# Earlier W_out weights, a reordered MLP entry, split right-factor buffers, and a rearranged first stage in a one-core transformer block

## The chip, the cores and the metric

The kernel runs on one core of one Trainium2 chip. The metric is device time in microseconds (us) of one execution, the median of several.

## The reference, cut to what matters

One transformer block on x of 1024 x 1024, float32 throughout:

```python
u = rms_norm(h, norm_mix_pre)
(q_n, kc_n, vc_n, ks_n, vs_n, kw_n, vw_n, g_n,
 q_s, k_s, v_s, gate_a, gate_b) = split(u @ w_in)
o_a = nsa_attention(...)          # compressed, selected and window branches
o_b = swa_sink_attention(...)
y = sigmoid(gate_a) * (o_a @ w_up_nsa) + sigmoid(gate_b) * (o_b @ w_up_swa)
h = h + rms_norm(y @ w_out, norm_mix_post)
u = rms_norm(h, norm_mlp_pre)
f = square(relu(u @ w_mlp_in)) @ w_mlp_out      # d_ff = 4096
h = h + rms_norm(f, norm_mlp_post)
```

## The kernel before, in words

TensorE multiplies in a reduced float32 type, so every operand is first split into a high and a low part (`split`: ScalarE rounds and copies, VectorE or GpSimd subtracts), and every product is three matmuls (high by high, high by low, low by high). Weights come from HBM in tiles called `wraw` and become `wh` and `wl`.

The work runs in six stages.

1. **First stage.** `x` comes in eight blocks of 128 rows (`xt`). Each is squared on ScalarE (line 283), scaled by its root mean square and by the norm weights `gB` on VectorE (line 285), transposed by TensorE and split into `uh` and `ul`. `gB` is the weight vector repeated on all partitions by a DMA (`load_bcast`). `v_weights` loads the columns of `w_in` for the values in eight row blocks (`vraw`, two buffers, three DMAs each); `v_block` multiplies a block of `u` by them. All of these loads stand in SyncE's queue.
2. **Projections and attention**, up to the output `o_d`, with the gate columns as filler for TensorE.
3. **Up-projection**, a loop over eight column groups `dc`, whose result `yh`, `yl` lies in pools on the right side of SBUF.
4. **W_out** (`out_proj`): four passes, each for two row blocks and all columns; each pass runs over eight row blocks `k2` of `w_out`, and each `k2` is 12 matmuls. Its weights go through the pool `wp2`, whose space on the left side is that of the attention output `oh_`, `ol_` that the up-projection reads to its last matmul. `norm_a`, `norm_b` and `norm_t` then make the MLP's normed input and transpose it.
5. **MLP entry and first MLP product.** The product is a seven-product (Strassen-Winograd) scheme over 2 x 2 blocks. The right factors `bh[i]`, `bl[i]` are sums of blocks of the input, made by `norm_t` (number 5) and `factor` (3, 6, 4, 7) on VectorE and ScalarE. `head` computes the two products that need only rows 0 to 511 (four `head`s run ahead of the rest, NPRE = 4) and stores `c11` to the DRAM scratch `f_d[0]`. `mlp1(p)` does the other five products of the column pair p (16 pairs); pairs 0 and 1 run interleaved with `factor`. Its left factors are sums of weight blocks: one sum (`sm`, line 1014) and three differences (line 1041) on GpSimd.
6. **Second MLP product** (`product`), again seven products, with split tiles `vh`, `vl`, `fh`, `fl` in the pool `st2` that lies where the right factors were, and the final norm.

The order of each engine's instructions is written at build time by a planner that simulates the engines; among the instructions it holds ready it takes them in the order of the program. `tc.issue_after(ins)` puts the block's instructions behind `ins` on the engine of `ins`. A tile that lies where an earlier tile lay waits until that tile's last reader is done. Queues are in order: an instruction of SyncE that waits holds every DMA behind it.

Of the kernel before, what the change touches and what calls it, by code (L numbers as in the profile page):

```python
# [52 lines left out]
def tile_hybrid_block(ctx: ExitStack, tc: tile.TileContext, x, norm_mix_pre, norm_mix_post, norm_mlp_pre,  # L53
# [27 lines left out]
    def load_bcast(dst, vec):  # L81
        nc.sync.dma_start(dst, bass.AP(tensor=vec.tensor, offset=vec.offset, ap=[[0, P], [1, vec.shape[-1]]]))
# [50 lines left out]
    load_bcast(sink, attn_sinks)  # L133
    nsink = const.tile([P, 8], F32, name="nsink")
    nc.vector.tensor_scalar(nsink, sink, -1.0, None, op0=ALU.mult)
# [36 lines left out]
    with ExitStack() as s_u:  # L172
# [36 lines left out]
        with ExitStack() as s:  # L209
# [12 lines left out]
            for pr, pos in zip(pos_r, (cmp_pos_k, cmp_pos_v)):  # L222
                nc.gpsimd.dma_start(pr, pos[0].rearrange("(a b) d -> a (b d)", b=2))

            def v_weights():
# [17 lines left out]
            with ExitStack() as s0:  # L243
                tp = s0.enter_context(pool("t0"))
                gB = tp.tile([P, D], F32, name="gB")
# [26 lines left out]
                for b in range(NB):  # L272
                    xt = tp.tile([P, D], F32, name="xt", tag="xt", bufs=4)
                    nc.sync.dma_start(xt, x[b * P:(b + 1) * P, :])
                    if b == 0:
                        load_bcast(gB, norm_mix_pre)
# [8 lines left out]
                    nc.vector.scalar_tensor_tensor(u, xt, r, gB, op0=ALU.mult, op1=ALU.mult)  # L285
# [456 lines left out]
    with ExitStack() as s:  # L742
# [3 lines left out]
        yl = [p.tile([P, NB, 512], F32R, name="yl", tag="yl") for p in yp]  # L746
        s_ps = s.enter_context(ExitStack())
        pp = s_ps.enter_context(pool("ps2", space=PSUM))
        ps_any = lambda: pp.tile([P, 512], F32, name="ps", tag="ps", bufs=6)
        with s_ot:  # L750
            dp = s_ot.enter_context(pool("dtmp"))
            for dc in range(8):
# [11 lines left out]
                for c in range(2):  # L764
# [11 lines left out]
                    split(yh[c][:, dc, :], yl[c][:, dc, :], t[0])  # L776
        s_w.close()
# [28 lines left out]
        we = s_we.enter_context(pool("we"))  # L806
        wor = w_out.rearrange("(k p) c -> p k c", p=P)
# [3 lines left out]
        started = []  # L811

        def out_proj(c, ts_, nhs, xs_=(), at=0):
            pss = {(t, nh): ps_any() for t in ts_ for nh in nhs}
            n = 1024 // (512 * len(nhs))
            for k2 in range(NB // n):
                wh, wl = load_w([(None, wor[:, n * k2:n * k2 + n, 512 * nhs[0]:512 * nhs[-1] + 512])],
# [452 lines left out]
```

## Time and profile before

| | |
|---|---|
| median of 3 runs | 1553.06 us (1552.43 to 1554.15) |
| the profiled execution | 1550.25 us |
| its span, first to last instruction | 1548.5 us |
| TensorE (PE) busy in the span | 1475.5 us, 95% |
| VectorE (DVE), ScalarE (ACT), GpSimd (POOL) busy | 1053.7, 788.3, 362.6 us |
| mean granted clock of TensorE | 0.985 of 2.4 GHz |

How to read the rows below. A row of the timeline has the start in us from the span's start, the duration in us, the engine, the line of the kernel, the operation, the tiles (out<-in), the shapes and how many instructions were merged (x8); in brackets stands how long the engine was idle before, and whose end released it. SPq is SyncE's queue. A row of a stretch has its bounds, its length, the busy us of PE, PEld (weight loads), DVE, ACT and POOL with the instructions counted, then TensorE's granted clock as a share, the DMA engines' busy share and GB/s. A row of a group of equal instructions has the line, the engine, the operation, the tiles and shapes, the count, the busy us, the mean ns of one, and the idle time before them.

### The profile page before, as it was taken

The page shows a single profiled execution, that of the slowest core. Times are in us where ns is not written, and L with a number is a line of the kernel's source. Part 1 is how long each engine was busy: PE and PEld are TensorE (multiplying, and loading weights), DVE is VectorE, ACT ScalarE, POOL GpSimd, SP SyncE. Part 2 cuts the span into 40 slices and gives each one's busy share as a digit, 9 for nine tenths or more (in the row PEclk, how much of TensorE's full clock was granted, in tenths as well). Part 3 has the DMA queues.
Part 4 walks back from the last instruction along what each step waited for, and adds up shares of the span by engine and source line. Part 5 has one row for each costly group of instructions (what it writes and reads, how often), then busy time and mean ns, then how long its engine had stood idle before and what let it go on. Part 6 is the DMA issues. An engine that isn't in the chain of part 4 may idle for free.

```text
span 1548.5 us, 19945 instructions
## 1 busy us (share of the span) xinstructions
PE 1475.5 (95%) x6920; PEld 1208.1 (78%) x6920; DVE 1053.7 (68%) x2086; ACT 788.3 (51%) x1525; POOL 362.6 (23%) x290
## 2 busy tenths in 40 slices
PE   6998999999999999999898969899999899999997
PEld 5897888788887788888766757688888688888886
DVE  5555774598855988646547798787667555594775
ACT  5344675598854988654346663233322334334533
POOL 3000342100001000041052035676556300000302
PEclk9999999999999999999999979999999999999999
DMA  7733125111132111174356633444444697353551
GB/s 218 252 98 87 35 50 158 46 35 41 36 99 61 40 35 42 32 257 148 108 192 233 221 116 107 155 148 166 157 137 144 220 359 270 99 194 102 164 176 55
DMA packets 162037, 204.79 MB, mean 132 GB/s; under 512 B 15120, under 2 KB 105264, under 8 KB 161936
## 3 DMA queue, kind: packets, MB, share of 16 engines
q1 hardware_dynamic: 154224, 180.68, 36.8%
q0 software_dynamic: 6992, 20.48, 3.8%
q10 hardware_dynamic: 720, 2.36, 0.4%
q8 instruction: 54, 0.88, 0.2%
q14 instruction: 47, 0.39, 0.1%
HBM read 153.02 MB, written 58.32 MB: 136 GB/s over the span
## 4 chain that ended last, share of the span: by engine, by line
PE 69%; issue 8%; DVE 6%; POOL 3%; DMA 2%; ACT 2%; DVEq 0%; POOLq 0%; ACTq 0%
PE xs L1167 10%; PE ys L1167 8%; PE mm L124 5%; PE mm L126 5%; PE mm L125 5%; PE ps L959 5%; PE ps L961 5%; PE ps L960 5%; PE pt L522 5%; PE o L535 2%; PE o L534 2%; PE s L489 2%; DMA wraw<-in_w_out_dram 2%; PE s L490 2%; PE ps L124 2%
## 5 line engine op out<-in xcount | busy, mean ns | idle before, releaser
L124 PE MATMUL mm<-uh,wh 128*128 128x512 f32 x464 | 200.2, 431 | 5.3 <-DVE qb L448 3.2
L125 PE MATMUL mm<-ul,wh 128*128 128x512 f32 x464 | 183.9, 396 | 0.0
L126 PE MATMUL mm<-uh,wl 128*128 128x512 f32 x464 | 183.7, 396 | 0.0
L91 DVE TENSOR_TENSOR tl<-pt,th 128x512 fp32r<-128x512 f32 x162 | 110.6, 687 | 42.1 <-ACT th L87 41.2
L91 POOL TENSOR_TENSOR wl<-wraw,wh 128x1024 fp32r<-128x1024 f32 x16 | 38.4, 2403 | 417.1 <-ACT wh L87 385.2
L502 ACT ACTIVATE e<-e,nm 128x256 f32<-128x256 f32 (+7 forms) x192 | 124.3, 649 | 20.0 <-DVE nm L496 19.5
L87 ACT ACTIVATE fh<-fraw 128x1024 fp32r<-128x1024 f32 x56 | 59.4, 1063 | 146.1 <-PE xs L1167 78.5
L87 ACT ACTIVATE wh<-wraw 128x1024 fp32r<-128x1024 f32 x69 | 73.1, 1059 | 113.9 <-PE mm L125 36.7
L87 ACT ACTIVATE th<-pt 128x512 fp32r<-128x512 f32 (+1 forms) x178 | 104.4, 593 | 50.6 <-PE pt L522 43.1
L91 DVE TENSOR_TENSOR fl<-fraw,fh 128x1024 fp32r<-128x1024 f32 x56 | 69.3, 1243 | 78.3 <-ACT fh L87 78.3
L1167 PE MATMUL xs<-vl,fh 128*128 128x512 f32 x256 | 100.7, 393 | 4.2 <-DVE vl L91 4.2
L126 PEld LDWEIGHTS mm<-uh,wl 128*128 128x128 f32 x464 | 87.4, 188 | 20.7
L124 PEld LDWEIGHTS mm<-uh,wh 128*128 128x128 f32 x464 | 88.0, 190 | 18.4 <-issue 3.3
L522 PE MATMUL pt<-ident,e 128*128 128x128 f32 x648 | 101.1, 273 | 0.3 <-DVE tl L91 0.2
L91 DVE TENSOR_TENSOR wl<-wraw,wh 128x1024 fp32r<-128x1024 f32 x53 | 69.7, 1315 | 46.0 <-ACT wh L87 45.8
L1167 PE MATMUL xs<-vh,fl 128*128 128x512 f32 x256 | 100.4, 392 | 0.0
L1167 PE MATMUL xs<-vh,fh 128*128 128x512 f32 x256 | 100.1, 392 | 0.0
L125 PEld LDWEIGHTS mm<-ul,wh 128*128 128x128 f32 x464 | 88.3, 190 | 11.9
L522 PEld LDWEIGHTS pt<-ident,e 128*128 128x128 f32 x648 | 80.7, 140 | 18.4 <-issue 0.9
L1190 POOL TENSOR_TENSOR cc<-cc,gB 128x512 f32<-128x512 f32 x14 | 24.3, 1762 | 268.9 <-ACT sq L1189 267.2
L87 ACT ACTIVATE ws_h<-wraw 128x512 fp32r<-128x512 f32 x48 | 30.1, 629 | 107.1 <-PE ps L960 104.8
L959 PE MATMUL ps<-bh,ws_h 128*128 128x512 f32 x192 | 76.3, 397 | 3.9 <-ACT ws_h L87 1.7
(287 smaller groups left out, 4046.4 us busy)
## 6 DMA issues: line engine op xcount, KB each, us to landing
fraw<-f_d SPq DMA_DIRECT2D x48, 512.0 KB, 3.5
wraw<-in_w_mlp_in_dram SPq DMA_DIRECT2D x36, 512.0 KB, 4.4
wraw<-in_w_out_dram SPq DMA_DIRECT2D x32, 512.0 KB, 3.6
f_d<-q SPq DMA_DIRECT2D x64, 256.0 KB, 3.7
b<-in_w_mlp_out_dram SPq DMA_DIRECT2D x32, 512.0 KB, 10.8
wraw<-in_w_in_dram SPq DMA_DIRECT2D x27, 512.0 KB, 4.6
f_d<-c SPq DMA_DIRECT2D x48, 256.0 KB, 4.3
gate_d<-gst SPq DMA_DIRECT2D x32, 256.0 KB, 2.0
```

The costliest lines, as they stand in the source:

```text
L87: nc.scalar.activation(h, src, AF.Copy)
L91: eng.tensor_tensor(l, src, h.bitcast(F32), op=ALU.subtract)
L124: nc.tensor.matmul(ps, ah, bh, start=first, stop=False)
L125: nc.tensor.matmul(ps, ah, bl, start=False, stop=False)
L126: nc.tensor.matmul(ps, al, bh, start=False, stop=last)
L489: nc.tensor.matmul(ps[:, :w], qs[r][:, qcol], kh, start=True, stop=False)
L502: nc.scalar.activation(e[:, :n], e[:, :n], AF.Exp, scale=-1.0, bias=nm[:, r:r + 1], accum_out=sm[:, r:r + 1])
L522: tr = nc.tensor.transpose(pt[:rows, r, :], es[r][:, off:off + rows], ident)
L959: nc.tensor.matmul(ps, ah[:, k, :], bh[i][:, k, :], start=n[0], stop=False, skip_group_check=True)
L960: nc.tensor.matmul(ps, ah[:, k, :], bl[i][:, k, :], start=False, stop=False, skip_group_check=True)
L961: nc.tensor.matmul(ps, al[:, k, :], bh[i][:, k, :], start=False, stop=n[1], skip_group_check=True)
L1167: nc.tensor.matmul(bank[t], l_[:, j, ts], r_[:, j, :], start=a_, stop=z_, skip_group_check=True)
```

## The change

Four groups of edits, of which the first three were joined and the fourth was added.

- **W_out.** Two row blocks of `w_out` are loaded during the up-projection (at dc = 5) into a new pool `wo` on the right side, and the first of them is split there. `out_proj`'s first pass takes them for k2 = 0 and 1; the pool `we` is opened after that pass.
- **MLP entry.** `norm_b(6)` and `norm_b(7)` stand before `norm_t(4)` instead of behind the first `head`; `factor(3, ...)` is put behind `norm_b(7)` on VectorE, and `factor(6, 4, 7)` behind the last subtraction of `norm_t` on VectorE and behind the copy `s1` on ScalarE. The squared ReLU of the four early `c11` moves from VectorE to ScalarE (two steps), and their stores from SyncE's queue to GpSimd's. The raw weights of pairs 0 to 3 are loaded ahead in one sequence, into tiles of `wp2` and `w1a`. The sum and differences of pairs 0 and 1 move from GpSimd to VectorE.
- **Right-factor placing.** Factors 5, 3, 6 lie in a pool of their own (`u1a`), 4 and 7 in `u1`; the split tiles of every fourth step of the second MLP product lie in a new pool `st3`, the others in `st2`.
- **First stage.** Blocks 1 and 2 of `x` go on ScalarE's queue; the norm weights come as one row (`gr`) and are spread to all partitions by two matmuls with a row of ones and two copies; block 0 is scaled in two halves; the value weights come two row blocks at a time and their low parts are all subtracted on VectorE; the sink load moves to GpSimd's queue and its negation to the end of the stage.

```diff
             def v_weights():
-                for k in range(NB):
-                    raw = wp.tile([P, NV], F32, name="vraw", tag="wraw", bufs=2)
-                    nc.sync.dma_start(raw[:, 0:128], wr[:, k, C_VS:C_VS + 128])
-                    nc.sync.dma_start(raw[:, 128:280], wr[:, k, C_VW:C_VW + 152])
-                    nc.sync.dma_start(raw[:, 280:408], wr[:, k, C_VB:C_VB + 128])
-                    split(vh[:, k, :], vl[:, k, :], raw, l_eng="pool" if k % 2 else "dve")
+                for k in range(0, NB, 2):
+                    raw = wp.tile([P, 2, NV], F32, name="vraw", tag="wraw", bufs=2)
+                    for a, b, c in ((0, 128, C_VS), (128, 280, C_VW), (280, 408, C_VB)):
+                        nc.sync.dma_start(raw[:, :, a:b], wr[:, k:k + 2, c:c + b - a])
+                    split(vh[:, k:k + 2, :], vl[:, k:k + 2, :], raw)
...
+                gr = tp.tile([1, D], F32, name="gr")
+                nc.scalar.dma_start(gr, norm_mix_pre)
+                one = tp.tile([1, P], F32, name="one")
+                nc.vector.memset(one, 1.0)
...
-                    nc.sync.dma_start(xt, x[b * P:(b + 1) * P, :])
+                    (nc.scalar if b in (1, 2) else nc.sync).dma_start(xt, x[b * P:(b + 1) * P, :])
                     if b == 0:
-                        load_bcast(gB, norm_mix_pre)
+                        for c in range(2):
+                            cs = slice(c * 512, (c + 1) * 512)
+                            ps = ps_x()
+                            nc.tensor.matmul(ps, one, gr[:, cs], start=True, stop=True)
+                            nc.vector.tensor_copy(gB[:, cs], ps)
...
-                    nc.vector.scalar_tensor_tensor(u, xt, r, gB, op0=ALU.mult, op1=ALU.mult)
+                    for cs in ((slice(0, 512), slice(512, D)) if b == 0 else (slice(0, D),)):
+                        nc.vector.scalar_tensor_tensor(u[:, cs], xt[:, cs], r, gB[:, cs], op0=ALU.mult, op1=ALU.mult)
...
+        def wo_load(k):
+            r = wo.tile([P, 1, 1024], F32, name="wraw", tag="wraw", bufs=2)
+            nc.sync.dma_start(r, wor[:, k:k + 1, :])
+            wo_raw.append(r)
...
+                if dc == 5:
+                    wo_load(0)
+                    wo_load(1)
+                    wo_hl += [wo.tile([P, 1, 1024], F32R, name=n, tag=n) for n in ("wh", "wl")]
+                    split(*wo_hl, wo_raw[0])
...
+        u1a = s_u2r.enter_context(pool("u1a", side="right"))
         u1 = s_u2r.enter_context(pool("u1", side="right"))
         for i in (5, 3, 6, 4):
-            bh[i] = u1.tile([P, 4, 512], F32R, name=f"bh{i}")
+            bh[i] = (u1 if i == 4 else u1a).tile([P, 4, 512], F32R, name=f"bh{i}")
...
+        norm_b(6)
+        norm_b(7)
         norm_t(4)
...
-            nc.vector.scalar_tensor_tensor(c11, c11, 0.0, c11, op0=ALU.max, op1=ALU.mult)
-            nc.sync.dma_start(f_d[0][p], c11)
+            if p < NPRE:
+                nc.scalar.activation(c11, c11, AF.Relu)
+                nc.scalar.activation(c11, c11, AF.Square)
...
+            (nc.gpsimd if p < NPRE else nc.sync).dma_start(f_d[0][p], c11)
...
-        for b in range(4):
-            factor(3, b)
+        with tc.issue_after(last_norm[0].ins):
+            for b in range(4):
+                factor(3, b)
...
+        raws = {p: load_raw(p) for p in range(NPRE)}
...
-            nc.gpsimd.tensor_tensor(sm, a21, a22, op=ALU.add)
+            diff = nc.vector if p < 2 else nc.gpsimd
+            with tc.issue_after(last_t[0].ins):
+                diff.tensor_tensor(sm, a21, a22, op=ALU.add)
...
-                nc.gpsimd.tensor_tensor(o, i0, i1, op=ALU.subtract)
+                diff.tensor_tensor(o, i0, i1, op=ALU.subtract)
...
+        def st_tile(name, kc):
+
+            p, n = (st3, 1) if kc % NG == NG - 1 else (st2, NG - 1)
+            return p.tile([P, 2, 512], F32R, name=name, tag=name, bufs=n)
```

## Rows read from the trace of the kernel before

**Rows 1.** Seven stretches of the span, all engines.

```profile
0.00:42.00 42.00, 27.70 (x119) 22.26 (x120) 24.88 (x57) 22.25 (x46) 12.48 (x18) 0.96 0.78 229
42.00:768.90 726.90, 715.06 (x3667) 597.80 (x3665) 492.42 (x1388) 456.26 (x1021) 95.42 (x94) 1.00 0.29 85
768.90:800.20 31.30, 25.70 (x97) 19.92 (x96) 8.84 (x11) 9.83 (x10) 13.11 (x8) 0.89 0.59 204
...
884.00:907.00 23.00, 22.94 (x104) 18.68 (x105) 22.61 (x46) 17.25 (x35) 1.06 (x2) 1.00 0.57 171
907.00:955.40 48.40, 34.81 (x138) 26.84 (x136) 40.24 (x52) 21.10 (x38) 20.66 (x14) 0.82 0.27 76
955.40:1025.00 69.60, 63.73 (x261) 49.12 (x261) 56.38 (x52) 20.51 (x34) 52.02 (x32) 0.98 0.46 152
...
1227.60:1238.00 10.40, 6.17 (x18) 4.56 (x18) 10.05 (x11) 1.96 (x3) 2.17 (x3) 0.67 0.61 180
```

**Rows 2.** Timeline of the first stage, all engines, us 0 to 42.

```profile
5.48 1.71 SPq L274 DMA_DIRECT2D xt<-in_x_dram  x2
5.49 1.06 ACT L283 ACTIVATE u<-xt 128x1024 f32<-128x1024 f32 x1 [3.25 <-DMA xt<-in_x_dram]
...
7.65 1.29 DVE L285 SCALAR_TENSOR_TENSOR u<-xt,rs_o,gB 128x1024 f32<-128x1024 f32 x1
...
9.08 1.94 PE L161 MATMUL pt<-ident,u 128*128 128x128 f32 x8 [9.08 <-DVE u L285]
...
19.60 0.46 PE L125 MATMUL s<-vl,uh 128*128 128x408 f32 x1 [1.71 <-DVE vl L91]
```

**Rows 3.** The chain that ended last, around the first W_out load.

```profile
768.31 3.94 DMA wraw<-in_w_out_dram
```

**Rows 4.** Timeline of PE in the first W_out pass.

```profile
773.44 2.07 PE L124 MATMUL ps<-wh,yh 128*128 128x512 f32 x4 [4.49 <-ACT wh L108]
...
778.73 1.47 PE L124 MATMUL ps<-wh,yh 128*128 128x512 f32 x4
...
787.50 1.10 PE L124 MATMUL ps<-wh,yh 128*128 128x512 f32 x4
...
790.30 1.10 PE L124 MATMUL ps<-wh,yh 128*128 128x512 f32 x4
```

**Rows 5.** Timeline of the MLP entry: SyncE's queue, GpSimd, VectorE and PE.

```profile
902.73 8.44 SPq L977 DMA_DIRECT2D f_d<-c  x3
...
911.21 34.85 SPq L1010 DMA_DIRECT2D wraw<-in_w_mlp_in_dram  x6
...
915.79 1.26 POOL L1014 TENSOR_TENSOR ws<-wraw 128x512 f32<-128x512 f32 x1 [14.06 <-DMA wraw<-in_w_mlp_in_dram]
...
911.34 1.28 DVE L864 SCALAR_TENSOR_TENSOR o<-hb,rs_o,gpre 128x1024 f32<-128x1024 f32 x1
...
912.76 1.94 PE L874 MATMUL pt<-ident,o 128*128 128x128 f32 x8 [4.72 <-DVE o L864]
...
918.95 0.79 PE L959 MATMUL ps<-bh,s_h 128*128 128x512 f32 x1 [4.25 <-ACT p L1019]
...
923.89 0.79 PE L961 MATMUL ps<-bh,s_l 128*128 128x512 f32 x1 [3.71 <-DVE s_l L91]
```

**Rows 6.** Groups of equal instructions on VectorE and ScalarE, us 884 to 940.

```profile
L91 DVE TENSOR_TENSOR bl<-braw,bh 128x512 fp32r<-128x512 f32 x8 | 7.5, 953 | 0.0
...
L896 DVE TENSOR_TENSOR braw<-b_l,braw 128x512 f32<-128x512 f32 x4 | 2.7, 679 | 0.0
...
L87 ACT ACTIVATE bh<-braw 128x512 fp32r<-128x512 f32 x8 | 4.9, 628 | 1.5 <-DVE braw L899 0.8 <-DVE braw L896 0.6
```

**Rows 7.** Timeline of VectorE and PE at the start of the second MLP product.

```profile
1227.92 0.69 DVE L1056 TENSOR_TENSOR c<-ps,p 128x512 f32<-128x512 f32 x1 [2.50 <-PE ps L961]
...
1229.85 1.22 DVE L91 TENSOR_TENSOR fl<-fraw,fh 128x1024 fp32r<-128x1024 f32 x1
...
1232.26 0.79 PE L1167 MATMUL xs<-vl,fh 128*128 128x512 f32 x1 [4.23 <-DVE vl L91]
```

More of the change, by code (lines that the diff above doesn't have):

```diff
@@ L746, in tile_hybrid_block @@
         yl = [p.tile([P, NB, 512], F32R, name="yl", tag="yl") for p in yp]
+        s_wo = s.enter_context(ExitStack())
+        wo = s_wo.enter_context(pool("wo", side="right"))
+        wor = w_out.rearrange("(k p) c -> p k c", p=P)
+        wo_raw, wo_hl = [], []
+        def wo_load(k):
+            r = wo.tile([P, 1, 1024], F32, name="wraw", tag="wraw", bufs=2)
+            nc.sync.dma_start(r, wor[:, k:k + 1, :])
+            wo_raw.append(r)
         s_ps = s.enter_context(ExitStack())
@@ L816, in out_proj @@
             for k2 in range(NB // n):
-                wh, wl = load_w([(None, wor[:, n * k2:n * k2 + n, 512 * nhs[0]:512 * nhs[-1] + 512])],
-                                [n, 512 * len(nhs)], *((wp2, 2) if not started else (we, WEB)), cut=CUT[c], rpool=wp2, l_eng="dve" if c else None)
+                if started or k2 > 1:
+                    wh, wl = load_w([(None, wor[:, n * k2:n * k2 + n, 512 * nhs[0]:512 * nhs[-1] + 512])],
+                                    [n, 512 * len(nhs)], *((we[0], WEB) if started else (wp2, 2)), cut=CUT[c],
+                                    rpool=wp2, l_eng="dve" if c else None)
+                elif k2:
+                    wh, wl = (wp2.tile([P, 1, 1024], F32R, name=n_, tag="w" + n_[1], bufs=2) for n_ in ("wh", "wl"))
+                    split(wh, wl, wo_raw[1])
+                else:
+                    wh, wl = wo_hl
                 if k2 == at:
@@ L830, in out_proj @@
                                 k == 0, k == NB - 1)
+            if not started:
+                s_wo.close()
+                we.append(s_we.enter_context(pool("we")))
             started.append(1)
@@ L882, in norm_t @@
             t1 = eh.tile([P, 4, P], F32, name="t1", tag="hb", bufs=2)
-            nc.vector.tensor_tensor(t1, pts[0], braw[b % 4, 0], op=ALU.subtract)
+            last_t[0] = nc.vector.tensor_tensor(t1, pts[0], braw[b % 4, 0], op=ALU.subtract)
             nc.scalar.activation(b12[:, :, bs], pts[0], AF.Copy)
@@ L985, in tile_hybrid_block @@
                 norm_t(5)
-                norm_b(6)
-                norm_b(7)
             if p == 1:
@@ L1002, in ab, with load_raw @@
                     p_.tile([P, 4, P], F32R, name=tag + "l", tag=tag + "l", bufs=bufs))
-        def mlp1(p):
-            raw = []
-            for e in range(2):
-                r = wp2.tile([P, NB, P], F32, name="wraw", tag="wraw", bufs=2) if e == 0 else \
-                    w1a.tile([P, NB, P], F32, name="wraw2", tag="wraw2", bufs=2)
-                c0 = (2 * p + e) * P
-                nc.sync.dma_start(r, w_mlp_in[:, c0:c0 + P].rearrange("(k p) c -> p k c", p=P))
-                raw.append(r)
+        def load_raw(p):
+            raw = {}
+            for e in (1, 0):
+                pool_, tag = ((w1a, "wraw2") if e else (wp2, "wraw")) if p > 3 else \
+                    ((wp2, "wraw"), (w1a, "wraw2"), (wp2, "w" + "hl"[e]), (wp2, "w" + "hl"[e]))[p]
+                raw[e] = pool_.tile([P, NB, P], F32, name="wraw", tag=tag, bufs=2)
+                c0 = (2 * p + e) * P
+                nc.sync.dma_start(raw[e], w_mlp_in[:, c0:c0 + P].rearrange("(k p) c -> p k c", p=P))
+            return raw
+        raws = {p: load_raw(p) for p in range(NPRE)}
+        def mlp1(p):
+            raw = raws[p] if p in raws else load_raw(p)
             a11, a12, a21, a22 = raw[0][:, 0:4], raw[0][:, 4:8], raw[1][:, 0:4], raw[1][:, 4:8]
             sm = w1a.tile([P, 4, P], F32, name="ws", tag="ws", bufs=3)
-            nc.gpsimd.tensor_tensor(sm, a21, a22, op=ALU.add)
+            diff = nc.vector if p < 2 else nc.gpsimd
+            with tc.issue_after(last_t[0].ins):
+                diff.tensor_tensor(sm, a21, a22, op=ALU.add)
             early = p in pre
@@ L1077, in tile_hybrid_block @@
                 next(g)
-            for b in range(4 if i else 0):
-                factor(i, b)
+            with tc.issue_after(last_t[0].ins), tc.issue_after(last_s1[0].ins):
+                for b in range(4 if i else 0):
+                    factor(i, b)
         for p in range(2, NPAIR):
@@ L1095, in tile_hybrid_block @@
         st2 = s.enter_context(pool("st2", side="right"))
+        st3 = s.enter_context(pool("st3", side="right"))
+        def st_tile(name, kc):
+            p, n = (st3, 1) if kc % NG == NG - 1 else (st2, NG - 1)
+            return p.tile([P, 2, 512], F32R, name=name, tag=name, bufs=n)
         pq = s.enter_context(pool("ps3", space=PSUM))
```

30 lines of the change are left out of this document (15 added, 15 removed).

## The prediction

> **What bounds the kernel now.** I read the table of stretches first. TensorE (PE) is the bound: in us 42 to 768.9 it is busy 715 of 727 [rows 1]. What a change can win is therefore its idle time and the time it spends at 1.2 GHz, and that sits in few places. The reader is to subtract the first busy figure from the length in each stretch: 14.3 us are idle in the first 42, 5.6 in the first W_out pass (768.9 to 800.2), 13.6 at the MLP entry (907 to 955.4), 5.9 in the pairs behind it, 4.2 at the start of the second MLP product. In three of these the granted clock is also low: 0.89, 0.82 and 0.67 [rows 1]. Then I read each place in the timeline, with the bracket that names who ended the wait.
>
> At full clock a group of 12 matmuls takes 790.30 - 787.50 = 2.80 us [rows 4]. I use this as the price of one W_out row block and of one product of the first MLP product, which are both 12 matmuls of 512 columns.
>
> **W_out.** PE waits 4.49 us for the first weights [rows 4]: their DMA starts only at 768.31, when the attention output under the buffer has been read, and takes 3.94 us [rows 3], then comes the split. After the wait the first 12 matmuls take 778.73 - 773.44 = 5.29 us instead of 2.80 [rows 4]: the clock has fallen, cost 2.5. The stretch of 31.3 us holds eight groups, 8 x 2.80 = 22.4, so at most 8.9 are to be won. The edit puts the first two row blocks into space that nobody holds. PE then goes on at 768.9 without a break for 5.6 us, to 774.5. The third block, which goes the old way, lands when the first one did (768.31 + 3.94 = 772.3) and needs one rounding copy before PE can start: about 773.4, in time. From there on loads and PE run side by side as they do now. That removes the wait (4.5) and the slow start (2.5): **7 us**. Lower bound 4, if the second block's split, which waits for the same old space, makes PE wait some 3 us at 771.7; upper 8.9. The two loads and one split inside the up-projection cost nothing: DMA engines are at 0.29 there and VectorE is busy 492 of 727 us [rows 1]; without that cover it would be the load's 3.9 us.
>
> **MLP entry.** In 907 to 955.4 PE has ten products (five each of pairs 0 and 1), 28.0 us, and two sets of eight transposes, about 2 us together at full clock (half of the 1.94 of the slow one for each [rows 5]). 48.4 - 30 = 18.4 us are lost. Three waits follow each other [rows 5]. The transposes of the last block wait 4.72 us for `norm_b(7)` on VectorE, which starts at 911.34 though PE was through at 907. The first product waits 4.25 and then 3.71 us for its left factor: GpSimd starts the sum at 915.79 because its raw weights were issued at 911.21, and they were issued then because SyncE's queue stood behind three stores of `c11` from 902.73 on. The rest is the low clock.
>
> The edits hit all three. `norm_b(7)` is no longer behind `factor(3)` and `factor(6)`, and can follow its sums: I put it at 897 to 902. The stores leave SyncE's queue, so the raw weights come as soon as a buffer is free, before 907. So the first product can start at about 909. What is late next is VectorE. It is full already: 22.6 of 23.0 us before 907 [rows 1], and it makes all the right factors. The edits take off four squared ReLUs (the shape of the 679 ns row [rows 6], 2.7 us) and put on two sums and six differences (8 x 0.68 = 5.4 us). ScalarE's eight extra steps are 8 x 0.63 = 5.0 us [rows 6] and just fit into the 5.75 us it has idle before 907 [rows 1]. What decides is how long VectorE's steps are: those that ran beside GpSimd's work average 953 ns against 679 [rows 6], 2.2 us for that group alone, and some 8 us over all groups of this kind between 884 and 940 by my estimate from the same ratio over 30 steps. The moved sums take GpSimd's work of pairs 0 and 1 away, but pairs 2 and 3, whose weights now come early, can put GpSimd's work back in the same place. The two ends: VectorE loses 5.3 us of work (- 2.7 + 5.4 - 8) and PE runs almost through, 18 us won; or it gains 2.7, and the right factors are ready no earlier than now, some 936 us, so that PE ends the last two products at about 942 to 945 and the gain is 10 to 13, and less if waits of 4 us each drop the clock again: 6. I take **11 us**, in the lower half, because VectorE's row before 907 shows no room.
>
> The Trainium skill ("SBUF — State Buffer", section "SBUF: two separate sides") has GpSimd and a VectorE step with two SBUF inputs exclude each other for a whole instruction. The 953 against 679 ns agree with that. By it alone, the moved steps take away all of the lengthening and the entry wins 18; with pairs 2 and 3 in their place it wins what rival 1 says.
>
> **The pairs behind.** In 955.4 to 1025 GpSimd is busy 52.0 of 69.6 us, far more than later, and PE idles 5.9 [rows 1]: GpSimd catches up with four pairs at once. With pairs 0 and 1 off it and the weights of 2 and 3 early, part of this goes. Between nothing and 5.9 I take **2 us**.
>
> **Right-factor placing.** PE waits 4.23 us at 1232.26 for `vl`; VectorE begins `fl` only at 1229.85, though it was idle 2.50 us until 1227.92 [rows 7]. The reason I read from the code: in the old placing `fl` lies where factor 7 lies, which the last product reads to its end. In the new one the first three steps' tiles lie on factors 5, 3 and 6, which are free one product (2.8 us) earlier, so `fl` and `vl` (1.22 us each) fit into that 2.50 us gap and behind it. The granted 0.67 over 10.4 us means 6.9 us at 1.2 GHz, 4.2 of them idle; the other 2.7 cost half, 1.3. In all 5.5; I take **5**, bounds 0 (the planner leaves them behind the last pair's sums) and 5.5.
>
> **First stage.** PE starts at 9.08: `x` lands, ScalarE starts at 5.49, and the scaling takes 1.29 before the transposes [rows 2]. Halving it for block 0 gives 0.6, and one load ahead of `x` less in SyncE's queue some 0.4. Blocks 1 and 2, issued at 5.48 so far [rows 2], go out in the first 3 us; the later idle time is 14.3 - 9.1 = 5.2, of which 1.71 is a wait for `vl` [rows 2] that GpSimd and VectorE shared. I take 1 + 2 = **3 us**. The copies of `gB` and the two matmuls lie in PE's and VectorE's empty first 5 us, the larger `vl` steps in VectorE's idle 17 us of 42 [rows 1]. Bounds: 1 + 5.2 = 6 above; below, a loss of 2.3, one block's transfer (0.52 MB at 229 GB/s [rows 1]), if blocks 1 and 2 push the first block back.
>
> The Trainium skill ("Trainium Kernel Development and Optimization", section "Key Constraints") says that DMAs of all queues share the same 16 engines, so a second queue saves only issue time. The DMA share of 0.78 in this stage bears on it but doesn't settle it; by it the term is 1, the sum 26, and rival 2 is the case.
>
> **The sum.** 7 + 11 + 2 + 5 + 3 = 28 us. The profiled execution took 1550.25, 1.75 more than its span and 2.8 less than the median of the runs shown. 1550.25 - 28 = 1522.3; against the median 1553.06 it is 1525.
>
> **The rivals.**
>
> 1. *VectorE takes the waits over at the entry* (0.20). PE starts the first product at 909 and then waits for factors 3 and 6. For it: 22.6 of 23.0 us busy, and 953 ns beside GpSimd. Against: GpSimd's steps of pairs 0 and 1 are gone. The entry wins 3, the pairs behind nothing: 28 - 8 - 2 = 18, 1535.
> 2. *The second queue gains nothing* (0.12). Blocks 1 and 2 delay block 0 by as much as the halves win, and the term of 3 turns to -1: 24 won, 1529. For it: 229 GB/s and 0.78 busy. Against: the repeated `gB` load of 0.52 MB is gone.
> 3. *W_out's loads set the pace anyway, or the early blocks come late* (0.06): the wait moves behind the second block; 28 - 7 = 21, 1532.
> 4. *All the waits go* (0.08): 8.9 + 18 + 5 + 5.5 + 3 = 40, 1513.
> 5. *Slower* (0.03). The planner writes each engine's order anew for the whole program. The place is the attention between 42 and 768.9, where 11.8 us are idle [rows 1]; the price is what a worse order of fillers adds there, and it decides from 28 us on, when that idle time passes 40; at 35 the result would be 1560. Nothing in the diff touches this stage, so little speaks for it.
>
> **How the numbers follow.** The forecast has 0.51, its own range is 1518 to 1532. The range of 8 in 10 takes in rival 4 on one side and most of rival 1 on the other, 1511 to 1539. A difference of 0.2% (3.1 us) is about what a measurement can tell from no change. Faster by more than that holds in all cases but the last, and fails in a tail of rival 1: 0.95; within 0.2%: 0.02; slower: 0.03.
>
> **What would show it.** PE idle at 769 under 1 us and clock 1.00 behind it; the last transposes of `norm_t(7)` before 905, the first product of pair 0 at 909 or so, and no wait over 2 us up to 945; no wait for `vl` at the first xs matmul; the first transposes before 8.5. It would be wrong if VectorE's order puts `norm_b(7)` late again, or if waits of 4 us reappear between the products of pairs 0 and 1.

## The result and the profile after

The changed kernel takes 1532.38 us, the median of 4 runs (1530.81 to 1533.55); the kernel before took 1553.61 us beside it (4 runs, 1552.43 to 1554.35). The ratio is 0.9863, with a 95% interval of 0.9846 to 0.988: 21 us faster. The forecast was 1525 with a range of 1511 to 1539. The time is inside the range, but the sum of 28 us was 7 too high, and it was spread wrongly over the places, with errors both ways that partly cancel.

The two profiled executions have spans of 1548.5 and 1531.3 us, 17.2 apart; the medians differ by more because the profiled execution of before was 3.4 us under its median and that of after 0.7 above. First the stretches of the changed kernel (columns as in [rows 1]). The first keeps the bound of 42 us and the pairs behind the entry keep the length of 69.6 us; the others are cut at the same points of the work as there:

```profile
0.00:42.00 42.00, 35.52 (x152) 27.07 (x153) 29.00 (x71) 22.49 (x44) 7.71 (x15) 1.00 0.85 252
...
763.90:791.10 27.20, 23.38 (x97) 17.62 (x96) 8.63 (x11) 8.74 (x10) 10.08 (x7) 1.00 0.61 207
...
898.90:949.90 51.00, 34.27 (x125) 25.27 (x124) 45.71 (x61) 25.85 (x45) 19.13 (x13) 0.80 0.32 88
949.90:1019.50 69.60, 69.60 (x301) 56.19 (x300) 57.86 (x58) 21.93 (x36) 52.79 (x34) 1.00 0.46 159
1215.30:1225.70 10.40, 10.35 (x39) 8.39 (x40) 10.33 (x13) 3.07 (x3) 1.51 (x3) 0.84 0.77 230
```

The idle time of TensorE (length less first busy figure) went from 14.3 to 6.5 us in the first 42 (3.75 of the difference are the new matmuls that spread the norm weights, before the first transposes), and from 5.9 to nothing in the pairs behind the entry. But at the entry 16.7 us are idle now, 51.0 - 34.27, where 13.6 were, and the clock is 0.80 where it was 0.82. The entry, from which most was forecast, is the place that got worse.

To see where the time came from, I took four points of TensorE's timeline from each trace: the end of the up-projection, the first matmul of the first `head`, the end of the first MLP product, the last `xs` matmul (`xs` are sums of the second MLP product). The lengths between them, in us, for all kernels of this study:

```
                start to end of   W_out, up to    first MLP   second MLP
                up-projection     first head      product     product
before              768.95          114.89         343.97       311.35
after               763.85          110.31         338.89       308.83
undo_first          772.35          109.96         338.37       308.87
undo_wout           765.18          113.64         340.14       307.73
undo_entry          765.68          107.45         343.90       308.03
undo_rf             763.59          109.95         335.32       311.31
sum1_late           764.70          110.06         337.11       307.24
raws23_late         763.66          110.58         336.37       307.51
diffs_pool          764.91          109.13         336.40       308.89
combo               764.60          110.24         336.51       308.01
combo2              764.81          113.07         337.89       307.24
one_queue           763.67          108.34         338.29       308.88
bcast_late          765.08          108.85         338.38       307.24
final3              762.83          108.54         335.35       308.79
```

After less before: 5.1 us from the first stage, 4.6 from W_out, 5.1 from the first MLP product, 2.5 from the second, 17.3 in all. The columns also show what one trace can carry: the same W_out code gives 107.5 to 113.1. Even so the kernels with the old code of a place stand apart: in every column the two longest are before and the kernel that turns that place back (768.95 and 772.35 against 762.8 to 765.7; 114.89 and 113.64 against at most 113.1; 343.97 and 343.90 against at most 340.1; 311.35 and 311.31 against at most 308.9). So each of the four parts earns something; the size of each is known to some 3 us.

**First stage.** The timeline of PE: the first transposes start at 8.51 instead of 9.08 [rows 2], and the wait of 1.71 us for `vl` at 19.60 is gone; the longest that is left is the 0.17 shown.

```profile
8.51 1.09 PE L159 MATMUL pt<-ident,u 128*128 128x128 f32 x4 [1.81 <-DVE rs_r L147]
...
12.36 0.71 PE L125 MATMUL s<-vl,uh 128*128 128x408 f32 x1 [0.17 <-DVE vl L91]
```

**W_out.** The timeline of PE in the first pass, and the chain that ended last there:

```profile
770.74 1.20 PE L124 MATMUL ps<-wh,yh 128*128 128x512 f32 x4 [1.34 <-ACT wh L108]
777.06 1.20 PE L124 MATMUL ps<-wh,yh 128*128 128x512 f32 x4 [0.45 <-ACT wh L108]
784.57 1.20 PE L124 MATMUL ps<-wh,yh 128*128 128x512 f32 x4 [1.64 <-ACT wh L108]
```

```profile
761.45 8.10 DMA wraw<-in_w_out_dram
...
769.63 1.07 ACT wh L108
...
770.76 1.67 POOL wl L116
772.44 3.40 DMA wraw<-in_w_out_dram
```

PE goes on at 763.7 without the wait of 4.49 us and at full clock [rows 4]. But the third row block takes 8.10 us to land, not 3.94 [rows 3], and then two buffers alternate: rounding 1.07, low part 1.67, next load 3.40 and more. The pass takes 27.1 us from its first matmul to the next pass, exactly what it took before, so W_out won the wait and nothing behind it: the slow first group is gone, and waits for loads (3.4 us in the rows above) have its place.

**MLP entry.** The timeline of VectorE, ScalarE and PE:

```profile
899.01 0.68 DVE L1065 TENSOR_TENSOR ws<-wraw 128x512 f32<-128x512 f32 x1
...
903.48 0.83 DVE L1065 TENSOR_TENSOR ws<-wraw 128x512 f32<-128x512 f32 x1 [3.79 <-DMA wraw<-in_w_mlp_in_dram]
904.24 1.88 DVE L930 TENSOR_TENSOR b_l<-b_l,b_h 128x512 f32<-128x512 f32 x3
...
906.04 0.68 DVE L1014 TENSOR_TENSOR c<-ps,s 128x512 f32<-128x512 f32 x1
...
907.41 0.63 ACT L1017 ACTIVATE c<-c 128x512 f32<-128x512 f32 x1
...
907.95 1.08 ACT L1070 ACTIVATE p<-ps 128x512 f32<-128x512 f32 x2
...
908.60 0.80 PE L998 MATMUL ps<-bh,s_h 128*128 128x512 f32 x1 [9.34 <-ACT p L1070]
...
919.29 0.79 PE L998 MATMUL ps<-bh,ws_h 128*128 128x512 f32 x1 [3.46 <-ACT ws_h L87]
...
931.46 6.88 DVE L91 TENSOR_TENSOR bh7l<-braw,bh7h 128x512 fp32r<-128x512 f32 x4
```

Read it backwards from the PE row at 908.60. PE waits 9.34 us for ScalarE's copies `p` (they take the heads' sums out of PSUM, the memory of TensorE's sums, before the first product adds to them). The copies stand behind the two steps of the fourth head's `c11`; these wait for VectorE's add at 906.04; and that stands behind VectorE's sum for pair 1 at 903.48, which waited 3.79 us for a raw weight. Neither the add nor the copies need that weight. The order made them need it.

```profile
895.00:901.00 6.00, 4.26 (x23) 3.33 (x22) 1.98 (x3) 3.62 (x8) 0.55 (x1) 1.00 1.05 285
901.00:907.00 6.00, 0.00 (x0) 0.00 (x0) 3.52 (x6) 1.64 (x4) 2.52 (x2) 0.53 0.92 252
```

```profile
893.15 10.31 DMA wraw<-in_w_mlp_in_dram
```

The two stretches of 6 us and the row of the chain show why the weight is late: the DMA engines are full (shares 1.05 and 0.92), because eight loads of 512 KB for four pairs go out in a row, and this load takes 10.31 us. By the semaphores in the trace (the counters that an instruction waits on) it is the fifth of the eight, though the program has it third; the fourth, which lands at 901.10, is the one that GpSimd's sum for pair 2 waits for. So the order of SyncE's queue has a part in it too.

**Second MLP product.** The wait for `vl` (4.23 us, [rows 7]) is gone, and a shorter one has come:

```profile
1212.85 1.22 DVE L91 TENSOR_TENSOR fl<-fraw,fh 128x1024 fp32r<-128x1024 f32 x1
1213.98 0.68 DVE L1107 TENSOR_TENSOR c<-ps,p 128x512 f32<-128x512 f32 x1
...
1214.70 0.60 ACT L1109 ACTIVATE c<-ps 128x512 f32<-128x512 f32 x1 [0.56 <-DVE c L1107]
...
1215.35 0.74 PE L1224 MATMUL xs<-vh,fh 128*128 128x512 f32 x1 [2.30 <-ACT c L1109]
```

### The profile page after: what moved, and what is told of

Its sections match the earlier page's. It is cut to its first block, busy times and chain, and to the rows that moved or that the text cites. A ratio compares the mean times of both kernels' runs of the same rounds, so it can differ in the third digit from the quotient of the medians.

```text
span 1531.3 us, 19921 instructions
## 1 busy us (share of the span) xinstructions
PE 1472.2 (96%) x6924; PEld 1205.1 (79%) x6924; DVE 1042.8 (68%) x2094; ACT 792.9 (52%) x1529; POOL 343.1 (22%) x281
## 4 chain that ended last, share of the span: by engine, by line
PE 81%; DVE 7%; DMA 6%; ACT 3%; issue 2%; POOL 1%; SPq 0%; DVEq 0%; ACTq 0%; POOLq 0%
PE xs L1224 10%; PE ys L1224 9%; PE mm L124 7%; PE mm L125 7%; PE mm L126 7%; PE ps L1000 6%; PE ps L998 6%; PE ps L999 6%; PE pt L532 5%; DMA wraw<-in_w_out_dram 4%; PE o L545 2%; PE o L544 2%; PE s L499 2%; PE s L500 2%; PE ps L126 2%
```

## The experiments

The changed kernel is the base of all of them; each states its edit.

**One part undone at a time.** Each turns back one of the four groups of the diff and keeps the other three:

```
undo_first:  first stage as before    (v_weights, gr, gB, xt, u, sink)
undo_wout:   W_out as before          (wo, wo_load, wo_hl, we)
undo_entry:  MLP entry as before      (norm_b, factor, c11, load_raw, sm, diff)
undo_rf:     one pool each, as before (u1a, st3)
```

> The changed kernel with its first stage as before. Theory (each part earns where the two traces differ at that place): the 5.2 us that the last x transposes came earlier are kept to the end, because TensorE is the bound from there on; so 1532.4 + 5.2 = 1537.6 us. Prediction's term for this part: 3 us, 1535.4. Rival (the two traces differ there by chance, a gain at the start is swallowed by the attention's fixed order): 1532 to 1533.

> The changed kernel with W_out as before (no early row blocks). Theory: the part earned 4.65 us by the traces, and loads set the pace from the third row block on; so 1532.4 + 4.7 = 1537.1 us, with a wait of about 4.5 us for the first weights and a low clock behind it back in the trace. Prediction's term: 7 us, 1539.4. Rival (loads set the pace anyway, nothing is earned): 1532 to 1533.

> The changed kernel with the MLP entry as before (order, sums, stores, raw weights), the other parts kept. Theory: entry and the pairs behind it together earned only 5.0 us (lost 4.1 at the entry, won 9.1 behind it); so 1532.4 + 5 = 1537.4 us. Prediction's terms: 11 + 2, so 1545.4. Rival (the entry's edit earns nothing once W_out's comes with it): 1532 to 1533.

> The changed kernel with the right factors and the split tiles of the second product in one pool each, as before. Theory: earned 2.5 us by the traces; 1532.4 + 2.5 = 1534.9 us, and the 4.2 us wait for the low part of the first right operand is back. Prediction's term: 5 us, 1537.4. Rival (the wait only changes its name, nothing earned): 1532 to 1533.

Measured: undo_first 1539.36 us (1535.96 to 1540.92), ratio to before 0.99 (0.9883 to 0.9916); undo_wout 1537.74 (1536.54 to 1538.31), 0.9891 (0.9876 to 0.9906); undo_entry 1537.24 (1536.47 to 1540.64), 0.9896 (0.9879 to 0.9913); undo_rf 1531.36 (1529.22 to 1531.99), 0.9849 (0.9834 to 0.9863). Against 1532.4 the parts are worth 7.0, 5.4, 4.9 and -1.0. By the ratios, each to before beside it, they are 5.7, 4.4, 5.1 and -2.2; the interval of a ratio is some 2.6 us to either side.

The first three lie within 1.8 us of the theory, and undo_wout has the wait for the first weights back (4.2 us); the entry's edit, forecast at 13 with the pairs behind it, earns 5. The table splits that: from the first head to the end of pairs 0 and 1 undo_entry needs 73.2 us (873.13 to 946.33) and the changed kernel 75.8 (874.16 to 949.99); behind it, to the end of the first MLP product, 270.7 against 263.1. The edit loses 2.6 at the entry and wins 7.6 behind it.

The total of undo_rf goes against the theory's 1534.9, and the places say why. Its second product takes 311.31 us, as before's 311.35; all kernels with the new placing take 307.2 to 308.9. So the placing earns 2.4 to 4.1 there. The wait for `vl` is back, at 2.5 us, not the 4.2 expected, and one of 1.5 us for a copy stands beside it. But the same kernel is 3.6 us shorter in the first MLP product, which that edit doesn't touch. The planner wrote another order:

```profile
897.89 0.69 DVE L1012 TENSOR_TENSOR c<-ps,s 128x512 f32<-128x512 f32 x1 [1.27 <-PE ps L998]
898.50 0.68 DVE L918 TENSOR_TENSOR t<-pt,braw 128x512 f32<-128x512 f32 x1
899.09 1.28 DVE L1063 TENSOR_TENSOR ws<-wraw 128x512 f32<-128x512 f32 x2
...
903.59 12.37 POOL L1063 TENSOR_TENSOR ws<-wraw 128x512 f32<-128x512 f32 x1 [6.33 <-DMA wraw<-in_w_mlp_in_dram]
```

Here the add for `c11` (line 1012 in this kernel) stands before the two sums, and the sums do not wait. But this is no test of VectorE's order alone, because SyncE's queue has another order too: by the semaphores the sum for pair 1 waits here for the fourth load, issued at 891.65 and landed at 899.50, not for the fifth, landed at 903.46. The next experiment changes VectorE's order on purpose.

One thing holds for the totals of the next seven kernels: their ratios (0.9848 to 0.9871) all lie in the interval of the changed kernel's (0.9846 to 0.988). None is shown to be faster by its total; what they show is read from the places.

**The order of one sum.**

```diff
-            with tc.issue_after(last_t[0].ins):
+            with tc.issue_after((last_c if p == 1 else last_t)[0].ins):
                 diff.tensor_tensor(sm, a21, a22, op=ALU.add)
```

`last_c` is the add that makes `c11`.

> The changed kernel with one order pinned: VectorE's sum for pair 1 is put behind the add that makes c11 of the fourth head; nothing else is edited. Theory (the entry lost because that sum, first in VectorE's order, waits 3.8 us for a late raw weight and holds the c11 add, the low part of factor 5 and with them ScalarE's copies that free the first product's PSUM): the first product of pair 0 starts at 904 to 905 instead of 908.6, the whole VectorE chain moves up by 3.8, time 1527.5 to 1529. Rival (VectorE's amount of work is the limit and the wait only fills a hole that it has anyway): the first product is earlier but the end of pairs 0 and 1 stays within 1 us of 950, time 1531.5 to 1533.

Measured: 1530.13 us (1529.55 to 1530.73), ratio 0.9853 (0.984 to 0.9867). The first product starts at 907.32, the pairs end at 948.83. This lies between the theory and the rival, and the first product is later than the theory's 904 to 905. VectorE's timeline shows what took the place of the wait:

```profile
900.21 4.03 DVE L930 TENSOR_TENSOR b_l<-b_l,b_h 128x512 f32<-128x512 f32 x3
904.16 0.68 DVE L1014 TENSOR_TENSOR c<-ps,s 128x512 f32<-128x512 f32 x1
904.76 0.68 DVE L1065 TENSOR_TENSOR ws<-wraw 128x512 f32<-128x512 f32 x1
...
900.70 1.32 POOL L1065 TENSOR_TENSOR ws<-wraw 128x512 f32<-128x512 f32 x1 [3.01 <-DMA wraw<-in_w_mlp_in_dram]
902.09 1.59 POOL L1092 TENSOR_TENSOR wraw<-wraw 128x512 f32<-128x512 f32 x1
```

The wait of 3.79 is gone, but three subtractions that took 1.88 us now take 4.03, because GpSimd's sum and difference for pair 2 run beside them. The wait had hidden these.

**The raw weights of pairs 2 and 3 later.**

```diff
-        raws = {p: load_raw(p) for p in range(NPRE)}
+        raws = {p: load_raw(p) for p in range(2)}
...
+            if i == 6:
+                with tc.issue_after(last_s1[0].ins):
+                    raws.update({p: load_raw(p, nc.scalar) for p in (2, 3)})
```

> The changed kernel with the four raw weight loads of pairs 2 and 3 taken out of the sequence that goes ahead and issued on ScalarE's queue behind the two s1 copies; those of pairs 0 and 1 as before. Theory (eight loads together fill the DMA engines, so the load that VectorE's sum for pair 1 waits for takes 10.3 us instead of 4 to 5): it lands in 5 to 6 us, the wait of 3.8 us goes, and GpSimd's early steps beside VectorE's go too; end of pairs 0 and 1 some 4 us earlier, and part of the 9 us won behind them is given back, because GpSimd starts pair 2 later: time 1529 to 1533. Rival (the load is late because its place comes free late, not because of the other loads): the wait stays over 3 us, time 1533 to 1536.

Measured: 1529.35 us (1529.27 to 1529.77), ratio 0.9849 (0.9835 to 0.9862), in the theory's range.

```profile
898.79 1.28 DVE L1065 TENSOR_TENSOR ws<-wraw 128x512 f32<-128x512 f32 x2
899.99 1.89 DVE L930 TENSOR_TENSOR b_l<-b_l,b_h 128x512 f32<-128x512 f32 x3
901.79 0.68 DVE L1014 TENSOR_TENSOR c<-ps,s 128x512 f32<-128x512 f32 x1
...
904.36 0.80 PE L998 MATMUL ps<-bh,s_h 128*128 128x512 f32 x1 [5.32 <-ACT p L1070]
...
917.23 0.80 PE L998 MATMUL ps<-bh,ws_h 128*128 128x512 f32 x1 [5.67 <-ACT ws_h L87]
```

VectorE's order in these rows is that of the changed kernel, sum for pair 1 first; only the loads are other. The sum doesn't wait, the first product starts 4.2 us earlier, the pairs end 3.5 earlier (946.51), and 1 us is given back behind. So the loads of pairs 2 and 3 are what made the weight late. They stood ahead of it and beside it: now it is the third load, issued at 890.46 and landed at 897.14, 2.7 us earlier out and 3.6 us shorter on its way. A new wait of 5.67 us stands at the third product.

**Sums and differences back on GpSimd.**

```diff
-            diff = nc.vector if p < 2 else nc.gpsimd
+            diff = nc.gpsimd
```

> The changed kernel with the sum and the three differences of pairs 0 and 1 back on GpSimd. Theory (VectorE is the bound from 904 to 945 and these eight steps are 5 us of it, but GpSimd beside it makes VectorE's steps 1.7 instead of 0.68 us): the two effects cancel within 3 us, the end of pairs 0 and 1 at 947 to 953, and GpSimd is later with pairs 2 and 3, so 1532 to 1537. Rival A (taking eight steps off VectorE is what helps): 1527 to 1530. Rival B (the prediction's low end: GpSimd's chain is the limit, first product at 912 or later): 1538 to 1541.

Measured: 1530.44 us (1527.43 to 1531.99), ratio 0.985 (0.9833 to 0.9866). Pairs 0 and 1 end at 944.23, 5.8 us earlier; 3.1 of these are given back in the pairs behind. The time is just above rival A's 1530: the entry goes its way, and what is given back behind it is the theory's. Moving eight steps to VectorE was a loss at the entry. The 5.8 us are not the price of the eight steps alone: the sum that waited is one of them, so the wait leaves VectorE too. Against raws23_late, where the wait is gone and the steps have stayed, the pairs end 2.3 us earlier.

**Both, and the other both.**

```
combo:   the order of one sum + raw weights of pairs 2 and 3 later
combo2:  diff = nc.gpsimd     + raw weights of pairs 2 and 3 later
```

> The changed kernel with both edits: pair 1's sum behind the c11 add of the fourth head, and the raw weights of pairs 2 and 3 on ScalarE's queue behind the s1 copies. Theory (the wait and GpSimd's early work beside VectorE are two costs; with the sum moved alone, GpSimd's sum of pair 2 stretched VectorE's three subtractions to 4.0 us and took the gain): without GpSimd there, the three subtractions take 1.9 us again, the first product of pair 0 starts at 903 or earlier, and the time is 1 to 2 us under that of the later loads alone: 1527.5 to 1528.5. Rival (VectorE's amount of work is the limit, both edits remove the same hole): 1529 to 1530.

> The changed kernel with the raw weights of pairs 2 and 3 on ScalarE's queue behind the s1 copies, and with sums and differences of pairs 0 and 1 back on GpSimd. Theory (VectorE is the bound from 904 to 945, and each of the two edits gives it back 2 to 3 us): if the two add up, 1527 to 1528. Rival (GpSimd's work for pairs 0 and 1 stretches VectorE's steps as much as it saves once pairs 2 and 3 are out of the way): 1529.5 to 1531.

Measured: combo 1530.25 us (1528.63 to 1533.51), ratio 0.9857 (0.9839 to 0.9875); combo2 1533.22 (1529.29 to 1535.32), 0.9871 (0.9853 to 0.9888). Neither adds up: combo is just above its rival's 1530, and combo2 is above its theory and its rival. In combo the three subtractions take 1.88 us again and the first product starts at 905.25, but then:

```profile
905.66 4.20 ACTq L1054 DMA_DIRECT2D wraw<-in_w_mlp_in_dram  x2
909.91 2.73 ACT L87 ACTIVATE bh<-braw 128x512 fp32r<-128x512 f32 x5 [4.22 <-DVE braw L934]
915.96 0.63 ACT L87 ACTIVATE s_h<-ws 128x512 fp32r<-128x512 f32 x1 [3.32 <-POOL ws L1065]
...
909.29 6.63 POOL L1065 TENSOR_TENSOR ws<-wraw 128x512 f32<-128x512 f32 x1 [3.91 <-DMA wraw<-in_w_mlp_in_dram]
...
920.95 0.79 PE L998 MATMUL ps<-bh,ws_h 128*128 128x512 f32 x1 [8.16 <-ACT ws_h L87]
```

The last two of these loads hold ScalarE's queue for 4.2 us, and five high parts of the right factors stand behind them. The row names a VectorE step as releaser, but it is the queue's row that ends at 909.86, just before they start. Then ScalarE loses 3.32 us more: the rounding `s_h` of pair 2 stands ahead of the `ws_h` that the third product needs, and it waits for GpSimd's sum, which takes 6.63 us (see the last section). combo2 lost 2.8 us in W_out, which its edits don't touch; its first MLP product (337.89) is no better than diffs_pool's (336.40).

**All of x on one queue.**

```diff
-                    (nc.scalar if b in (1, 2) else nc.sync).dma_start(xt, x[b * P:(b + 1) * P, :])
+                    nc.sync.dma_start(xt, x[b * P:(b + 1) * P, :])
```

> The changed kernel with all blocks of x on SyncE's queue; the rest of the first stage as changed. Theory (the first stage's 5 to 7 us come from the repeated norm weights no longer being loaded in 128 copies and from larger value weight steps; the second queue is a small part): 1 to 2 us lost, 1533 to 1535. Rival (the second queue is what brings blocks 1 and 2 early): 4 to 6 us lost, 1536 to 1539, with TensorE idle in front of the second block's transposes. Prediction's second rival (the queue gains nothing): 1532 to 1533.

Measured: 1528.96 us (1525.56 to 1533.62), ratio 0.9848 (0.9827 to 0.9868): no loss, and below all three forecasts. The last transposes of `x` do come 5.0 us later (65.15 against 60.12). The stretch from 90 to 165 us gives 3.9 of them back; the changed kernel first, then this one:

```profile
90.00:165.00 75.00, 70.15 (x315) 60.44 (x315) 36.58 (x72) 28.82 (x55) 1.04 (x2) 0.98 0.31 83
```

```profile
90.00:165.00 75.00, 74.00 (x342) 64.30 (x341) 42.61 (x79) 34.59 (x64) 2.25 (x2) 1.00 0.35 93
```

TensorE is idle 4.85 us there in the changed kernel (the longest wait is 3.2 us for `qb`) and 1.0 us with one queue. The orders of the two differ from the first stage on, so I can't say how much of the 5.0 is the queue and how much the order; what is shown is that the queue, as placed, earns nothing at the end.

**The repeated norm weights behind the first W_out blocks.**

```diff
-        load_bcast(gpost, norm_mix_post)
-        load_bcast(gpre, norm_mlp_pre)
...
+                if k2 == 5 and not started:
+                    load_bcast(gpost, norm_mix_post)
+                    load_bcast(gpre, norm_mlp_pre)
```

> The changed kernel with the two repeated norm weight loads (0.5 MB each), which stand in SyncE's queue ahead of the third and fourth row block of W_out, put behind the sixth block of the first pass in the program. Theory (those two and the two row blocks go out together, so the third row block takes 8.1 us to land instead of some 4, and the two buffers then keep a pace of 3.3 us a block): the third row block lands by 766.5, the waits of 1.3 and 1.6 us go, the first pass ends 2 to 3.5 us earlier, time 1529 to 1530.5. Rival (the two buffers' chain of load, split and release sets the pace by itself, wherever it starts): the first wait goes and comes back later in the pass, less than 1 us won, 1531.5 to 1532.5.

Measured: 1530.15 us (1526.73 to 1531.11), ratio 0.985 (0.9835 to 0.9865). The first pass takes 24.8 us instead of 27.1. It is in the theory's range. The first wait is gone, and the two others are 1.25 us together instead of 2.09:

```profile
779.57 1.20 PE L124 MATMUL ps<-wh,yh 128*128 128x512 f32 x4 [0.54 <-ACT wh L108]
783.34 1.20 PE L124 MATMUL ps<-wh,yh 128*128 128x512 f32 x4 [0.71 <-ACT wh L108]
```

The pass varies much between traces: from 25.0 to 30.8 us over the ten kernels that have the early blocks and the old place of the two loads. The two kernels with the new place have the two lowest, 24.8 and, below, 24.0. So the loads ahead are a part of the slow pace, 2.3 us against the changed kernel's trace, though undo_entry comes to 25.0 with the old place; the rest of the waits is the chain of two buffers.

**The three that were not slower, together.**

```
final3:  raw weights of pairs 2 and 3 later + norm weights behind the W_out blocks + x on one queue
```

> The changed kernel with the three edits that were not slower: raw weights of pairs 2 and 3 issued behind the s1 copies, the two repeated norm weights behind the first blocks of W_out, all blocks of x on SyncE's queue. Theory (three places that do not touch each other: entry 3.0, W_out 2.2, attention's order 3.4 by the medians): between 1524 (all add up) and 1527 (only the entry's 3.0 and W_out's waits of some 2 count, the queue of x is neutral). Rival (the differences of 2 to 3 us are what any new order of the planner gives, up or down): 1529 to 1533, no better than each alone.

Measured: 1526.7 us (1523.3 to 1528.2), ratio 0.9832 (0.9815 to 0.9848). It beats the kernel before by 26 us and the changed kernel by 5.7 by the medians; the intervals of the two ratios touch at 0.9846 to 0.9848. It is in the theory's range and under the rival's. By the table it is 1.0, 1.8 and 3.5 us shorter than the changed kernel in the first three stretches. The first product starts at 901.35 and the longest wait left at the entry is

```profile
917.58 0.79 PE L999 MATMUL ps<-bh,ws_h 128*128 128x512 f32 x1 [8.64 <-ACT ws_h L87]
```

As in combo, ScalarE waits there for GpSimd's sum of pair 2, 4.68 us.

## Why the prediction was right and wrong, point by point

- **Faster, inside the range**: right, though 0.4 us above the forecast's own narrower range (1518 to 1532). That TensorE's idle time is what can be won, and where it lies, held: all four places changed. That the total came out so near is in part luck: by the traces the entry fell 15 us short of its term, and the pairs behind and the first stage came out 9 above theirs.
- **W_out, 7 us**: the mechanism was right for the wait (4.49 us gone, clock 1.00), the size was not: 4.6 by the traces, 5.4 by undo_wout. The step that failed is that the third block "lands when the first one did" and is "in time". It took 8.10 us to land, since four loads of 512 KB (two norm weights, two row blocks) stood together, and from there the two buffers set the pace. That is rival 3 in part. Of the 8.9 us that the stretch seemed to offer, what the low clock cost was taken over by waits for loads.
- **MLP entry, 11 us**: wrong, and of the other sign: -4.1 by the traces (first head to the end of pairs 0 and 1: 883.84 to 955.54 before, 874.16 to 949.99 after), -2.6 by undo_entry. All three waits of [rows 5] were removed as the working said: `norm_b(7)` ends before 892, the last transposes stand at 898.66, the raw weights are issued from 883 on. The step that failed is that "the first product can start" 2 us after the heads (907 and 909 in the working). It started 9.8 after them (898.83 to 908.60), because I asked when its inputs are ready and not what stands ahead of them in VectorE's order. The moved sum brought a DMA wait into a full in-order engine. raws23_late shows the loads as the cause of that wait; sum1_late shows that moving the sum behind the add removes it, and that little is won by it. The prediction's own sign, "no wait over 2 us up to 945", failed with the waits of 9.34 and 3.46.
- **Rival 1 (VectorE takes the waits over, 3 + 0 for these two terms)** was the nearer one: 5.1 by the traces, where the forecast had 13; but it had nothing for the pairs behind, where all of the gain is. VectorE is busy 45.7 of 51.0 us at the entry, and removing its one long wait moved the end of the pairs by 1.2 us (sum1_late) or 3.5 (raws23_late); with the wait and the eight steps gone it moved by 5.8 (diffs_pool). How much of the loss is the amount of VectorE's work and how much its lengthening beside GpSimd is not separated.
- **That pairs 2 and 3 "can put GpSimd's work back in the same place"** is what happened, and the working had it only as a possibility: `bh7l`, four steps, takes 6.88 us instead of 2.7 (4 x 0.68).
- **The pairs behind, 2 us, bound 5.9**: 9.2 by the traces, 7.6 by undo_entry, above my bound. The bound took only the idle time of a row. The row below has 16 products, 192 matmuls (two more reach into it at its ends). They took 53.9 us; at 2.80 for 12 they take 44.8, so 9.1 were lost, part of them while PE counted as busy:

```profile
955.40:1009.30 53.90, 48.03 (x194) 36.38 (x194) 41.40 (x38) 14.58 (x24) 38.64 (x24) 0.97 0.47 153
```

- **Right-factor placing, 5 us**: 2.5 by the traces, 2.4 to 4.1 by the second product's lengths. `vl` is in time, as worked out; but the split steps now stand in VectorE's order ahead of the last pair's subtraction, and the first `xs` matmul waits 2.30 us for ScalarE's copy behind it. A wait took the place of the wait.
- **First stage, 3 us**: 5.1 by the traces, 7.0 by undo_first (8.5 in its trace). The wait for `vl` went, as forecast. The term of 1 us for the first block was too high: 0.57 here, and in the ten traces with this first stage the first transposes start between 8.38 and 9.02, against 9.08 and 9.09 with the old one. The term of 2 us for the later idle time was too low: behind the first transposes TensorE is idle 1.7 us up to 42, where it was 5.2, so 3.5 went. The old stage's low clock (0.96, 1.00 now) is not what was missing, for undo_first has the old stage at 1.00. What makes up the rest of the 5.1 stays open. Of rival 2 the mechanism did not occur, since block 0 was not delayed; its heading, that the second queue gains nothing, is borne out by the end of one_queue, not by its first stage.

The Trainium skill ("Trainium Kernel Development and Optimization", section "Key Constraints") says that several queues only save issue time, since they share the DMA engines. The end time of one_queue agrees with it; the 5.0 us at the last transposes do not speak for it, and the changed order keeps this open.

## What to carry to other kernels

When work moves onto an in-order engine, list what stands behind it there and what it waits for: a step that waits for a DMA belongs behind everything that doesn't need that data. Loads that were brought forward together each landed late here; bring forward only what is needed first. A planner that rewrites the order after every edit moved other places by up to 4 us here, so judge an edit by the length of its own stretch, not by the total alone, and by more than one trace of it. A step that waits for a slower engine belongs behind what others wait for, too: in combo and final3 a rounding for pair 2 held ScalarE.

## What the runs showed of the hardware

GpSimd and VectorE kept each other out for longer than the kernel before had shown. While GpSimd's sums and differences follow each other, VectorE's steps with two inputs in SBUF (the memory of the tiles) take 1.7 us instead of 0.68, one of each engine in turn. A GpSimd step that starts among VectorE's steps can fare much worse: in undo_rf its sum of pair 2 took 12.37 us (row above), where the same sum takes 1.25 in the changed kernel, at 901.17, while VectorE waits. From 903.59 on VectorE had one step with two SBUF inputs after the other without a gap; its first step that reads PSUM starts at 914.75, and GpSimd's sum ends 1.2 us later:

```profile
914.14 0.68 DVE L931 TENSOR_TENSOR braw<-b_l,braw 128x512 f32<-128x512 f32 x1
914.75 0.68 DVE L1086 TENSOR_TENSOR p<-ps,p 128x512 f32<-128x512 f32 x1
915.35 1.16 DVE L1090 TENSOR_TENSOR wraw<-wraw,ws 128x512 f32<-128x512 f32 x1
```

It is not a single case. In combo the same sum takes 6.63 us (row above) and in final3 7.85, and both end 1.2 us after the start of VectorE's first step that reads PSUM (914.73 and 912.02).

```profile
905.37 7.85 POOL L1066 TENSOR_TENSOR ws<-wraw 128x512 f32<-128x512 f32 x1 [3.75 <-DMA wraw<-in_w_mlp_in_dram]
...
912.02 0.68 DVE L1089 TENSOR_TENSOR p<-ps,p 128x512 f32<-128x512 f32 x1
```

In raws23_late it takes only 2.42 us among VectorE's steps; what decides which engine goes next stays open.

The Trainium skill ("SBUF — State Buffer", section "SBUF: two separate sides") says that the one that starts first holds the shared port for the whole instruction and the other is blocked. The 1.7 us and the end of the long wait agree with it; that many short steps in a row can keep the other side out for 11 us is what undo_rf adds, with combo and final3 behind it.
